# Seven block products for the last product of both layers of a decoder trunk, with the low halves of the weights made by adding DMAs

## The chip, the core and the metric

The kernel runs on one core of one Trainium2 chip. The metric is the device time of one execution in microseconds, the median of 3 runs. TensorE (PE) multiplies, VectorE (DVE), ScalarE (ACT) and GpSimd (POOL) do the elementwise work, and DMAs are started from SP's queue and from POOL's queue. All arithmetic is float32; a product of two float32 matrices is made of three products of "float32r" halves (below).

## The reference, cut to what matters

Two layers over x (1024 tokens by 1024 channels), each with a norm that is modulated by a vector c, a mixer, and a gated sum with x. Only the end of each mixer concerns the change:

```python
def even_mixer(h, ...):                       # layer 0
    ya = rg_lru(causal_depthwise_conv(xa, conv_w, conv_b), ...) * jax.nn.silu(ga)
    ...
    yb = stick_breaking_attention(q, k, v).reshape(bsz, slen, SB_WIDTH) * jax.nn.silu(gb)
    return jnp.concatenate([ya, yb], axis=-1) @ w_out          # 2048 x 1024

def odd_mixer(h, ...):                        # layer 1
    u, g = jnp.split(h @ w_in, 2, axis=-1)
    y = jax.nn.gelu(s5_ssm(u, ...))
    y = y * jax.nn.sigmoid(y @ glu_w + glu_b)
    return (y * jax.nn.silu(g)) @ w_out                        # 1024 x 1024
...
    x = x + gate * out                        # after each layer
```

In layer 0, `concatenate([ya, yb]) @ w_out` is the sum of a product with ya and one with yb, each 1024 x 1024 x 1024. The SSM of layer 1 needs rotation tables (powers of complex numbers on the unit circle, 32 of them by 128 steps on 128 partitions), which depend on parameters alone.

## The kernel before, in words

Activations lie feature by token: eight tiles of 128 features by 1024 tokens. A product with a 1024 x 1024 weight is made in eight output tiles m ("projections"). Each factor is split into a high half (a cast to float32r, line 72, on ACT) and a low half (the value less its high half, line 75, on DVE), and for each of eight k there are six matmuls of 512 tokens (lines 120 to 125): high weight by high and low activation, low weight by high activation, for two halves of the tokens. So a projection is 48 matmuls, and a whole product 384. A weight tile comes by SP into `w_raw` (two buffers), is split into `w_hi`, `w_lo` (two buffers each), and `w_next` asks for one tile ahead. The low half of the tile for projection m+2 can only be made once projection m has ended.

A second way of making a 1024 x 1024 product stands at the end of layer 1 (lines 1495 to 1559). Weights and activations are cut into 2 x 2 blocks (weights by even and odd output tile pairs, tokens in two halves), seven sums or differences of blocks are multiplied instead of eight blocks, and the results are put together (a Strassen-Winograd form). For each pair of output tiles u = 0..3 there are seven products of 4 x 3 matmuls (`st_mm`, lines 197 to 199): 84 matmuls, 336 in all. `st_x` (line 150) makes the seven right factors of a pair j of activation tiles: four differences on DVE, high halves on ACT, low halves on DVE. `st_w` (line 168) makes the seven left factors of u: sums and low halves on POOL (lines 181 to 189), high halves on ACT. For u = 0 the products run interleaved, j by j, in seven PSUM banks; for u > 0 one after the other.

Layer 0 ends in `out_even`: eight projections with ya, then eight with yb, each followed by `residual` (line 1159: x1 tile plus gate times the bank, two DVE instructions). yb comes back from DRAM in eight pieces through the `w_raw` buffers and is split. Beside the projections with yb, each finished x1 tile is scaled and split for layer 1 (lines 1181, 1182), stored by POOL's queue (1184) and squared for the next norm (1189, 1190). Eight `rotations` (line 1204 on) build the rotation tables on DVE, four instructions to a level, levels of 1, 2, 4, ... columns, in chunks of at most 32, and store them by POOL's queue.

PE's order is the order of the code. On the other engines a scheduler sets the order, except at the very start of the program, which is written out (a "manual schedule" names engines that take the order of the code). An engine waits at the head of its queue; what stands behind waits too.

Of the kernel before, what the change touches and what calls it, by code (L numbers as in the profile page):

```python
# [17 lines left out]
P = 128  # L18
# [32 lines left out]
GB = 2  # L51
LRU_ORDER = "gt0 ga1 cv1 cv2 ga2 gt1 dc0 cv3 gt2 ga3 xa4 cv4 gt3 dc0 xa5 cv5 gt4 xa6 cv6 ga4 gt5 dc0 xa7 cv7 gt6 ga5 gt7 dc0 ga6 ga7"


class Trunk:
# [33 lines left out]
    def shifted(self, raw):  # L89

        v = self.nc.vector
        out = self.h1p.tile([P, P], F32, name="wsh", tag="wsh", bufs=2)
        self.wsh.append(out)
        for k in range(KT):
            x, s = raw[:, k * P:(k + 1) * P], self.mod[:, 24 + k:25 + k]
            if k == 0:
                v.tensor_scalar(out, x, s, 0.0, op0=ALU.mult, op1=ALU.add)
            else:
                v.scalar_tensor_tensor(out, x, s, out, op0=ALU.mult, op1=ALU.add)

    def w_fetch(self, n):

        while self.w_loaded < min(len(self.w_order), n):
            hi = self.wp.tile([P, 1024], F32R, name="w_hi", tag="whi", bufs=2)
            lo = self.wp.tile([P, 1024], F32R, name="w_lo", tag="wlo", bufs=2)
            raw = self.load_split(self.w_order[self.w_loaded], hi, lo)
            if self.w_loaded in self.w_shifted:
                self.shifted(raw)
# [41 lines left out]
    def st_x(self, hi, lo, a, b, t):  # L150
# [3 lines left out]
        b2 = b.rearrange("p (c n) -> p c n", c=2)  # L154
        v.tensor_sub(t[:, 0], a[:, h1], a[:, h0])
        act.copy(hi[:, 0], a[:, h0])
        v.tensor_sub(t[:, 2], b[:, h1], a[:, h1])
        act.copy(hi[:, 1:3], b2)
        v.tensor_sub(t[:, 1], b[:, h1], t[:, 0])
        v.tensor_sub(t[:, 3], b[:, h0], t[:, 1])  # L160
        v.tensor_sub(lo[:, 0], a[:, h0], hi[:, 0].bitcast(F32))
        v.tensor_sub(lo[:, 1:3], b2, hi[:, 1:3].bitcast(F32))
        for i in (0, 2, 1, 3):
            act.copy(hi[:, 3 + i], t[:, i])
            v.tensor_sub(lo[:, 3 + i], t[:, i], hi[:, 3 + i].bitcast(F32))

    def st_w(self, src0, src1, place, t):

        nc = self.nc
        act, pool = nc.scalar, nc.gpsimd  # L170
        a = []
        for src in (src0, src1):
            raw = self.rp.tile([P, 1024], F32, name="w_raw", tag="raw")
            nc.sync.dma_start(raw, src)
            r = raw.rearrange("p (j e m) -> p e j m", e=2, m=P)
            a += [r[:, 0], r[:, 1]]
        s1, s2, s3, s4 = t[:, 0], t[:, 1], t[:, 2], t[:, 3]
        out = []
        for i, x in enumerate((a[0], s2, a[1], s3, s1, a[3], s4)):
            if i == 1:  # L180
                pool.tensor_tensor(s1, a[2], a[3], op=ALU.add)
                pool.tensor_tensor(s2, s1, a[0], op=ALU.subtract)
            elif i == 3:
                pool.tensor_tensor(s3, a[0], a[2], op=ALU.subtract)
            elif i == 6:
                pool.tensor_tensor(s4, a[1], s2, op=ALU.subtract)
            hi, lo = place(i)
            act.copy(hi, x)
            pool.tensor_tensor(lo, x, hi.bitcast(F32), op=ALU.subtract)
            out.append((hi, lo))  # L190
        return out
# [32 lines left out]
    def run(self):  # L224
# [12 lines left out]
        for half in range(2):  # L237
            self.w_order += [I["woe"][m][:, half * 1024:(half + 1) * 1024] for m in range(8)]
        self.s5_order = self.plan_s5()
        self.w_odd, self.w_shifted, self.wsh = len(self.w_order), set(), []  # L240
# [903 lines left out]
    def out_even(self):  # L1144
        nc, I = self.nc, self.I
        v = nc.vector
        x1p = self.pool("x1")
        x1 = self.x1 = x1p.tile([P, KT, T], F32, name="x1")
        ybp = self.pool("yb")
        ybh = ybp.tile([P, KT, T], F32R, name="yb_hi")  # L1150
        ybl = ybp.tile([P, KT, T], F32R, name="yb_lo")
        self.pair_i = 3
        ya = (self.yah, self.yal)

        def residual(m, ps):
            gate = self.mod[:, 16 + m:17 + m]
            for h in range(2):
                hs = slice(h * 512, (h + 1) * 512)
                v.scalar_tensor_tensor(x1[:, m, hs], ps[h], gate, x1[:, m, hs], op0=ALU.mult, op1=ALU.add)
# [3 lines left out]
        for m in range(8):  # L1163
            residual(m, self.proj(self.pair(), self.w_next(), ya))
            self.load_split(self.yb_s[m], ybh[:, m, :], ybl[:, m, :])
        self.yap2.release()
        self.yap.release()
        op = self.pool("oe")
        acc = op.tile([P, T], F32, name="acc")
        self.rot_s = [self.tc.dram_tile([P, 2, 4, P], F32, name=f"rot_s{m}") for m in range(8)]  # L1170
        self.h1p = self.pool("h1", side="right")
        self.h1h = self.h1p.tile([P, KT, T], F32R, name="h1_hi")
        self.h1l = self.h1p.tile([P, KT, T], F32R, name="h1_lo")
        self.rstd1 = self.h1p.tile([P, T], F32, name="rstd1")
        self.w_shifted.update(range(self.w_odd, self.w_odd + 3))
        self.x1_s = [self.tc.dram_tile([P, T], F32, name=f"x1_s{m}") for m in range(8)]
        for m in range(8):
            ps = self.proj(self.pair(), self.w_next(), (ybh, ybl))
            residual(m, ps)
            g = self.gain[:, 8 + m:9 + m]  # L1180
            nc.scalar.activation(self.h1h[:, m, :], x1[:, m, :], AF.Identity, scale=g)
            v.scalar_tensor_tensor(self.h1l[:, m, :], x1[:, m, :], g, self.h1h[:, m, :].bitcast(F32),
                                   op0=ALU.mult, op1=ALU.subtract)
            nc.gpsimd.dma_start(self.x1_s[m], x1[:, m, :])
            if m == 0:
                nc.scalar.activation(acc, x1[:, m, :], AF.Square)
            else:
                sq = op.tile([P, T], F32, name="sq1", tag="sq")
                nc.scalar.activation(sq, x1[:, m, :], AF.Square)
                v.tensor_add(acc, acc, sq)  # L1190
            self.rotations(m, op)
        self.acc = acc
        self.oe_pools = (op, ybp)
# [445 lines left out]
```

## Time and profile before

| | |
|---|---|
| three runs | 1343.68, 1343.10, 1342.44 us, median 1343.1 |
| the profiled execution | 1343.34 us, of which the span of the profile is 1341.3 us |
| PE busy | 1316.6 us (98%), 7020 matmuls, granted clock 0.999 |
| DVE, ACT, POOL busy | 1010.6, 651.8, 228.9 us |
| projections with ya, with yb | start at 767.5 and 856.2 us; the next product starts at 943.3 us |
| seven-product stage at the end | 1257.0 us to 1337.0 us |

The profiled execution lies 0.24 us above the median and 2.0 us above its own span. Busy shares are averages; a change in one stage is read from the rows of that stage. A matmul of 512 columns is listed with about 390 ns because its end is modelled; the distance from one start to the next is the pace.

### The profile page before, as it was taken

The numbers are of one execution on the slowest core, as the hardware profiler recorded it, in microseconds if no ns is written. First come the engines' busy times: TensorE is split into PE (matmuls) and PEld (weight loads), VectorE is DVE, ScalarE is ACT, GpSimd is POOL, SyncE is SP. The second block draws the span as 40 slices with busy tenths as digits, with TensorE's granted clock in tenths as the row PEclk, the third lists the DMA queues.
The fourth block names the chain that finished last, engine by engine and source line by source line (L and its number), as shares of the span: only waits on it lengthen the run. The fifth ranks groups of instructions, "written<-read, shape, count | busy, mean of one in ns | idle before, by whom it ended". The sixth has DMA issues, their size and how long they took to land.

```text
span 1341.3 us, 18939 instructions
## 1 busy us (share of the span) xinstructions
PE 1316.6 (98%) x7020; PEld 1137.7 (85%) x7020; DVE 1010.6 (75%) x1826; ACT 651.8 (49%) x1218; POOL 228.9 (17%) x411
## 2 busy tenths in 40 slices
PE   7998999999999999999999999999999999999998
PEld 3898989898999999988878878888888888888777
DVE  7949977777787868787999787866588669755653
ACT  6545454545454545455998621132463434632421
POOL 1012322222222222210000000000000000000784
PEclk9999999999999999999999999999999999999999
DMA  8443141414141414213112164342458778444331
GB/s 324 166 149 95 58 142 37 146 34 145 34 145 34 147 33 158 85 63 110 36 40 67 61 230 136 115 145 99 135 164 247 229 246 245 122 163 133 108 112 76
DMA packets 73356, 168.22 MB, mean 125 GB/s; under 512 B 9552, under 2 KB 35408, under 8 KB 73264
## 3 DMA queue, kind: packets, MB, share of 16 engines
q1 hardware_dynamic: 62256, 128.40, 31.3%
q0 software_dynamic: 11008, 38.62, 7.8%
q8 instruction: 55, 0.90, 0.3%
q14 instruction: 37, 0.30, 0.1%
HBM read 126.16 MB, written 40.83 MB: 125 GB/s over the span
## 4 chain that ended last, share of the span: by engine, by line
PE 78%; DVE 13%; ACT 3%; issue 3%; DMA 2%; POOL 1%; DVEq 0%; ACTq 0%; POOLq 0%
PE bank L120 6%; PE bank L121 6%; PE bank L123 6%; PE bank L122 6%; PE bank L124 6%; PE bank L125 6%; PE bank L771 6%; PE bank L773 6%; PE bank L772 6%; PE bank L837 2%; PE bank L199 2%; PE bank L197 2%; PE bank L198 2%; DMA ada_raw<-ada 2%; PE bank L849 1%
## 5 line engine op out<-in xcount | busy, mean ns | idle before, releaser
L771 PE MATMUL bank<-wqkv_hi,h_hi 128*128 128x384 f32 x512 | 173.6, 339 | 0.0
L773 PE MATMUL bank<-wqkv_hi,h_lo 128*128 128x384 f32 x512 | 172.3, 337 | 0.0
L772 PE MATMUL bank<-wqkv_lo,h_hi 128*128 128x384 f32 x512 | 172.3, 337 | 0.0
L72 ACT CAST w_hi<-w_raw 128x1024 fp32r<-128x1024 f32 x60 | 63.0, 1050 | 193.5 <-PE bank L123 148.5
L75 DVE TENSOR_TENSOR w_lo<-w_raw,w_hi 128x1024 fp32r<-128x1024 f32 x60 | 73.0, 1218 | 41.2 <-ACT w_hi L72 41.1
L771 PEld LDWEIGHTS bank<-wqkv_hi,h_hi 128*128 128x128 f32 x512 | 96.6, 189 | 0.3
L772 PEld LDWEIGHTS bank<-wqkv_lo,h_hi 128*128 128x128 f32 x512 | 96.6, 189 | 0.4
L773 PEld LDWEIGHTS bank<-wqkv_hi,h_lo 128*128 128x128 f32 x512 | 96.5, 189 | 0.0
L120 PE MATMUL bank<-h_hi,w_hi 128*128 128x512 f32 x224 | 89.1, 398 | 0.0
L122 PE MATMUL bank<-h_hi,w_hi 128*128 128x512 f32 x224 | 87.6, 391 | 0.8 <-DVE xc L1014 0.8
L124 PE MATMUL bank<-h_hi,w_lo 128*128 128x512 f32 x224 | 87.7, 392 | 0.4 <-DVE w_lo L75 0.4
L121 PE MATMUL bank<-h_lo,w_hi 128*128 128x512 f32 x224 | 87.7, 391 | 0.0
L123 PE MATMUL bank<-h_lo,w_hi 128*128 128x512 f32 x224 | 87.5, 390 | 0.0
L125 PE MATMUL bank<-h_hi,w_lo 128*128 128x512 f32 x224 | 87.4, 390 | 0.0
L778 ACT ACTIVATE nat<-bank 128x128 f32<-128x128 f32 x64 | 17.7, 277 | 141.3 <-PE bank L773 137.9
L826 DVE TENSOR_TENSOR_SCAN keep<-keep,diag 128x1024 f32<-128x1024 f32 (+3 forms) x64 | 86.2, 1347 | 0.1
L314 POOL TENSOR_SCALAR ss<-ss 128x2 f32<-128x2 f32 x64 | 28.6, 446 | 296.6 <-ACT nat L779 296.1
L820 ACT ACTIVATE keep<-bank,ss 128x512 f32<-128x512 f32 (+2 forms) x96 | 54.5, 597 | 21.7 <-PE bank L819 20.1
L783 DVE SCALAR_TENSOR_TENSOR nat<-bank,ss,gqk 128x128 f32<-128x128 f32 x64 | 22.1, 345 | 47.9 <-PE bank L837 25.9
L823 ACT ACTIVATE beta<-bank,ss 128x512 f32<-128x512 f32 (+3 forms) x96 | 54.4, 600 | 0.0
L290 DVE SCALAR_TENSOR_TENSOR ada_raw<-ada_raw,cs 128x1024 f32<-128x1024 f32 x39 | 47.6, 1220 | 7.8 <-DMA ada_raw<-ada 7.5
L315 POOL TENSOR_TENSOR ss<-ss,mh 128x2 f32<-128x2 f32 x64 | 51.9, 810 | 5.3
(436 smaller groups left out, 3739.2 us busy)
## 6 DMA issues: line engine op xcount, KB each, us to landing
ada_raw<-ada SPq DMA_DIRECT2D x39, 512.0 KB, 3.9
w_raw<-wqkv SPq DMA_DIRECT2D x21, 512.0 KB, 3.6
w_raw<-wfm SPq DMA_DIRECT2D x20, 512.0 KB, 3.6
w_raw<-woe SPq DMA_DIRECT2D x16, 512.0 KB, 3.8
w_raw<-wod SPq DMA_DIRECT2D x16, 512.0 KB, 4.4
x<-xT SPq DMA_DIRECT2D x8, 512.0 KB, 7.1
cx_s<-ce POOLq DMA_DIRECT2D x16, 256.0 KB, 2.7
win_s<-wsb POOLq DMA_DIRECT2D x16, 256.0 KB, 3.5
```

Of the source, the lines that this page charges most:

```text
L72: nc.scalar.copy(hi, raw)
L75: nc.vector.tensor_sub(lo, raw, hi.bitcast(F32))
L120: nc.tensor.matmul(ps[0], wh[:, k, :], rh[k][:, h0], start=first, stop=False)
L121: nc.tensor.matmul(ps[0], wh[:, k, :], rl[k][:, h0], start=False, stop=False)
L122: nc.tensor.matmul(ps[1], wh[:, k, :], rh[k][:, h1], start=first, stop=False)
L123: nc.tensor.matmul(ps[1], wh[:, k, :], rl[k][:, h1], start=False, stop=False)
L124: nc.tensor.matmul(ps[0], wl[:, k, :], rh[k][:, h0], start=False, stop=last)
L125: nc.tensor.matmul(ps[1], wl[:, k, :], rh[k][:, h1], start=False, stop=last)
L771: nc.tensor.matmul(ps[:, 0:384], hh[:, k, ts], wqh[:, ks], start=(k == 0), stop=False)
L772: nc.tensor.matmul(ps[:, 0:384], hh[:, k, ts], wql[:, ks], start=False, stop=False)
L773: nc.tensor.matmul(ps[:, 0:384], hl[:, k, ts], wqh[:, ks], start=False, stop=(k == KT - 1))
L826: v.tensor_tensor_scan(rev, rev, self.diag[:, T - n:T][:, ::-1], 0.0, op0=ALU.mult, op1=ALU.max)
```

## The change

Layer 0's product with yb is now made of seven block products too, and both layers share one function, `strassen`. In it, and from one projection ahead of it, the order of DVE, ACT, POOL and SP is that of the code. For u = 0 five products (4, 5, 0, 1, 2) run interleaved over the first three j, then the rest; for u > 0 the order is 4, 5, 0, 1, 3, 2, 6. The sums of weight blocks are made on DVE. For the low half of a left factor ACT writes the high half, then the source once more with scale -1 into the low half's place (which is cast, so it holds the negative of the high half), and POOL's queue starts a DMA that adds the unsplit block onto it: from DRAM for plain blocks, from SBUF for sums. No compute instruction of POOL is left at the end of the program.

The activations' factors of layer 0 are made from yb directly: pairs 0 and 1 beside the projections with ya, pairs 2 and 3 around the last of them. The stores of x1 and of the output are started by SP instead of POOL (but for the last pair's). Layer 1's input product takes its halves from tiles that the factors leave free; three small products with the shift vector (`shifted`) get loads of their own. The rotation tables are built in batches: the first five levels for 16 at once (`rotations_small`), the last two for four at once without chunks, beside the projections with ya.

```diff
-    def st_x(self, hi, lo, a, b, t):
+    def st_x(self, z, a, b, t):
...
+        for i in range(7):
+            act.copy(z[i][:, 0], x[i])
+        for i in range(7):
+            v.tensor_sub(z[i][:, 1], x[i], z[i][:, 0].bitcast(F32))
     def st_w(self, src0, src1, place, t):
...
-            hi, lo = place(i)
-            act.copy(hi, x)
-            pool.tensor_tensor(lo, x, hi.bitcast(F32), op=ALU.subtract)
+        v.tensor_add(s1, a[2], a[3])
+        v.tensor_sub(s2, s1, a[0])
+        v.tensor_sub(s4, a[1], s2)
+        v.tensor_sub(s3, a[0], a[2])
+        x = ((a[0], d[0]), (s2, s2), (a[1], d[1]), (s3, s3), (s1, s1), (a[3], d[3]), (s4, s4))
...
+        def make(*factors):
+            for i in factors:
+                ws[i] = hi, lo = place(i)
+                hf, lf = [y.rearrange("p j m -> p (j m)") for y in (hi, lo)]
+                act.copy(hf, x[i][0])
+                act.activation(lf, x[i][0], AF.Copy, scale=-1.0)
+                nc.gpsimd.dma_start(lf, x[i][1], accum_op=ALU.add)
+    def strassen(self, base, first, w_load, x, tile, gate, scratch, during, after):
...
+        ws, make = first
+        for u in range(4):
...
+            if u == 0:
+                order = [(i, j) for j in range(3) for i in (4, 5, 0, 1, 2)] + [(i, 3) for i in (4, 5, 0, 1)]
+                order += [(3, j) for j in range(4)] + [(2, 3)] + [(6, j) for j in range(4)]
+                for i, j in order:
+                    self.st_mm(b[i], ws[i], x(i, j), j, j == 0, j == 3)
+                p1, p6, p2, p7, p5, p4, p3 = b
+            else:
+                make(3, 6)
+                after(u - 1)
...
+            product(4, p5)
+            product(5, p4)
+            product(0, p1)
+            add(xb[:, h1], p5, gb)
+            if u == 0:
+                add(xa[:, h1], p5, ga)
...
+            add(xb[:, h0], p4, gb)
+            if u < 3:
+                ws, make = w_load(u + 1)
+                during(u)
+                if u == 0:
+                    make(4, 5)
+                    nc.scalar.copy(s1, p1)
+                    make(0, 1, 2)
+                else:
+                    nc.scalar.copy(s1, p1)
+                    make(4, 5, 0, 1, 2)
...
+            product(1, p6)
+            v.tensor_add(u2, p6, s1)
...
+            product(3, p7)
...
+            product(2, p2)
+            add(xa[:, h0], p2, ga)
+            product(6, p3)
+            add(xa[:, h1], p3, ga)
+        after(3)
     def out_even(self):
...
+        for m in range(6):
             residual(m, self.proj(self.pair(), self.w_next(), ya))
...
+            if m in (0, 1):
+                yb_factors(m)
+            if m in (1, 3):
+                small[m // 2] = self.rotations_small(m // 2, rotp)
+            for r in ((), (0, 1), (2, 3), (4, 5), (6,), (7,))[m]:
+                self.rotations(r, rotp, small[r // 4])
...
+        with self.tc.manual_schedule(engines={eng.DVE, eng.Activation, eng.Pool, eng.SP}):
+            first = w_load(0)
+            first[1](4, 5, 0, 1, 2)
+            self.proj(p7, w7, ya)
...
+            yb_factors(2)
+            residual(7, p7)
+            first[1](3, 6)
+            yb_factors(3)
+            self.strassen(0, first, w_load, x, lambda m: x1[:, m, :], gate,
...
     def layer1(self):
...
+            first = w_load(0)
+            first[1](4, 5, 0, 1, 2)
+            self.proj(p7, w7, (yh, yl))
+            sg = gate_tile(7)
+            z_factors(2)
+            v.tensor_mul(y[:, 7, :], gated(7, p7), sg)
+            first[1](3, 6)
+            z_factors(3)
+            self.strassen(4, first, w_load, x, tile, lambda m: self.mod[:, 40 + m:41 + m], lambda: scratch("x"),
```

What the scheduler makes of DVE beside the second and third projection with ya: before, the sums of projection 1 (banks 71 and 72), then the weight's low half for projection 3, then pieces of a rotation (`rot`).

```order
L1159 SCALAR_TENSOR_TENSOR x_7271<-bank_71,mod,x_7271 128x512
L1159 SCALAR_TENSOR_TENSOR x_7271<-bank_72,mod,x_7271 128x512
L75 TENSOR_TENSOR w_lo<-w_raw,w_hi 128x1024
L1216 TENSOR_TENSOR rot_7954<-rot,uw 128x8x8
L1217 TENSOR_TENSOR rot_7955<-rot,uw 128x8x8
L75 TENSOR_TENSOR yb_lo<-w_raw,yb_hi 128x1024
```

And now, at the same place of DVE's queue; `yb_raw` are the two yb tiles of pair 1, `st_x` their differences, `z` the right factors.

```order
L1260 SCALAR_TENSOR_TENSOR x_7271<-bank_71,mod,x_7271 128x512
L1260 SCALAR_TENSOR_TENSOR x_7271<-bank_72,mod,x_7271 128x512
L155 TENSOR_TENSOR st_x<-yb_raw_7439 128x512
L156 TENSOR_TENSOR st_x<-yb_raw_7441,yb_raw_7439 128x512
L157 TENSOR_TENSOR st_x<-yb_raw_7441,st_x 128x512
L162 TENSOR_TENSOR z<-yb_raw_7439,z 128x512
L158 TENSOR_TENSOR st_x<-yb_raw_7441,st_x 128x512
L162 TENSOR_TENSOR z<-yb_raw_7441,z 128x512 x2
L162 TENSOR_TENSOR z<-st_x,z 128x512 x4
L1398 TENSOR_TENSOR rot<-rot_7495,rot_7496 128x4x32
L76 TENSOR_TENSOR w_lo<-w_raw,w_hi 128x1024
```

The same low half `w_lo` now stands behind the eleven instructions for the factors of pair 1 and a piece of a rotation.

POOL at the beginning of layer 1's seven products, before: sums (`st_w`) and low halves computed.

```order
L181 TENSOR_TENSOR st_w<-w_raw 128x512
L184 TENSOR_TENSOR st_w<-w_raw 128x512
L182 TENSOR_TENSOR st_w<-st_w,w_raw 128x512
L189 TENSOR_TENSOR w_lo<-st_w,w_hi 128x512
L189 TENSOR_TENSOR w_lo<-w_raw,w_hi 128x512
L186 TENSOR_TENSOR st_w<-w_raw,st_w 128x512
```

And now: DMAs that add a sum (`st_w`) or a block of the weight in DRAM (`woo`).

```order
L191 DMA w_lo<-st_w 128x512
L191 DMA w_lo<-woo 128x512 x2
L191 DMA w_lo<-st_w 128x512
L191 DMA w_lo<-woo 128x512
L191 DMA w_lo<-st_w 128x512 x3
```

The subtractions have left POOL; in their place are transfers, of which the first five belong to u = 0's products 4, 5, 0, 1, 2.

DVE ahead of layer 1's first products, now: the gating of activation tile 6, the product of gate 7 with its activation (`gsr`), the factors of pair 2, and only then the gating of tile 7.

```order
L1680 TENSOR_TENSOR x_7271<-sgl,gsr 128x1024
L1674 TENSOR_TENSOR gsr<-gsr,x_7271 128x1024
L155 TENSOR_TENSOR st_x<-x_7271 128x512
L156 TENSOR_TENSOR st_x<-x_7271 128x512
L157 TENSOR_TENSOR st_x<-x_7271,st_x 128x512
L158 TENSOR_TENSOR st_x<-x_7271,st_x 128x512
L162 TENSOR_TENSOR z<-x_7271,z 128x512 x3
L162 TENSOR_TENSOR z<-st_x,z 128x512 x4
L1714 TENSOR_TENSOR x_7271<-sgl,gsr 128x1024
```

`gsr` has one buffer instead of two, so its load for tile 7 waits until tile 6 is gated, and everything below it in this list waits for that load.

## Rows read from the trace of the kernel before

**Rows 1.** The page, part 1: busy time, share of the span, instructions.
```profile
span 1341.3 us, 18939 instructions
...
PE 1316.6 (98%) x7020; PEld 1137.7 (85%) x7020; DVE 1010.6 (75%) x1826; ACT 651.8 (49%) x1218; POOL 228.9 (17%) x411
```
**Rows 2.** Busy time by stretch, matmuls alone: projections with yb, seven-product stage.
```profile
core 0: us, PE busy (x) PEld busy (x) DVE busy (x) ACT busy (x), PEclk, DMA share, GB/s
856.23:943.32 87.09, 87.09 (x386) 72.07 (x384) 11.29 (x17) 0.00 (x0) 1.00 0.32 109
1257.01:1337.04 80.03, 77.98 (x337) 62.76 (x335) 18.00 (x25) 3.60 (x6) 1.00 0.33 104
```
**Rows 3.** Timeline of PE: start, length, instruction. First u = 0, then u = 3.
```profile
1262.05 0.39 PE L199 MATMUL bank<-z_hi,w_lo 128*128 128x512 f32 x1
...
1266.85 0.39 PE L199 MATMUL bank<-z_hi,w_lo 128*128 128x512 f32 x1
...
1332.65 0.39 PE L199 MATMUL bank<-z_hi,w_lo 128*128 128x512 f32 x1
...
1336.81 0.40 PE L199 MATMUL bank<-z_hi,w_lo 128*128 128x512 f32 x1
```
**Rows 4.** Timeline of PE: where it waits in the seven-product stage.
```profile
1259.18 0.50 PE L199 MATMUL bank<-z_hi,w_lo 128*128 128x512 f32 x1 [0.85 <-POOL w_lo L189]
...
1279.15 0.50 PE L199 MATMUL bank<-z_hi,w_lo 128*128 128x512 f32 x1 [1.21 <-POOL w_lo L189]
```
**Rows 5.** Timeline of PE: the projections with ya begin, and their one wait.
```profile
767.47 0.40 PE L120 MATMUL bank<-ya,w_hi 128*128 128x512 f32 x1
...
778.07 0.50 PE L121 MATMUL bank<-ya_slot,w_hi 128*128 128x512 f32 x1 [0.57 <-DVE rot L1205]
```
**Rows 6.** Timeline of DVE beside projections 1 and 2 with ya.
```profile
777.97 0.06 DVE L1204 MEMSET rot<- 128x4 f32 x1
...
780.23 0.18 DVE L1216 TENSOR_TENSOR rot<-rot,uw 128x32 f32<-128x32 f32 x1
...
780.85 0.23 DVE L1216 TENSOR_TENSOR rot<-rot,uw 128x64 f32<-128x64 f32 x1
...
781.57 0.29 DVE L1216 TENSOR_TENSOR rot<-rot,uw 128x128 f32<-128x128 f32 x1
...
783.81 0.43 DVE L1216 TENSOR_TENSOR rot<-rot,uw 128x256 f32<-128x256 f32 x1
...
785.13 0.43 DVE L1216 TENSOR_TENSOR rot<-rot,uw 128x256 f32<-128x256 f32 x1
...
793.28 1.40 DVE L1159 SCALAR_TENSOR_TENSOR x<-bank,mod,x 128x512 f32<-128x512 f32 x2
794.92 1.23 DVE L75 TENSOR_TENSOR w_lo<-w_raw,w_hi 128x1024 fp32r<-128x1024 f32 x1 [0.24 <-ACT w_hi L72]
```
**Rows 7.** Timeline of DVE while right factors are made, POOL idle, then POOL at work.
```profile
1197.97 1.89 DVE L165 TENSOR_TENSOR z_lo<-st_x,z_hi 128x512 fp32r<-128x512 f32 x3
...
1256.71 4.66 DVE L165 TENSOR_TENSOR z_lo<-st_x,z_hi 128x512 fp32r<-128x512 f32 x4
```
**Rows 8.** Groups of ACT and DVE by shape: busy us, mean ns, idle before.
```profile
L188 ACT CAST w_hi<-st_w 128x512 fp32r<-128x512 f32 x16 | 9.7, 619 | 24.8 <-POOL st_w L182 14.1 <-POOL st_w L186 6.6 <-PE bank L198 3.2
...
L1504 DVE SCALAR_TENSOR_TENSOR x<-bank,mod,x 128x512 f32<-128x512 f32 x18 | 13.2, 747 | 18.2 <-PE bank L199 17.4 <-ACT st_x L1517 0.7
```
**Rows 9.** DMA issues: queue, count, KB each, median us from issue to landing.
```profile
w_raw<-yb_s SPq DMA_DIRECT2D x8, 512.0 KB, 3.8
...
win_s<-wsb POOLq DMA_DIRECT2D x16, 256.0 KB, 3.5
...
gsr<-gs_s SPq DMA_DIRECT2D x8, 512.0 KB, 4.4
...
out<-x POOLq DMA_DIRECT2D x7, 512.0 KB, 5.2
...
out<-x POOLq DMA_DIRECT2D x1, 256.0 KB, 2.3
```

More of the change, by code (lines that the diff above doesn't have):

```diff
@@ new lines, in st_w, with st_places, place @@
+        return ws, make
+    def st_places(self, pool):
+        two = {}
+        def place(i):
+            if i in (2, 4, 5):
+                return [pool.tile([P, 4, P], F32R, name=f"w{i}_{x}", tag=f"w{i}_{x}", bufs=1 + (i == 2)) for x in ("hi", "lo")]
+            k = i // 3
+            if k > 0:
+                k, i = 1, i // 6
+            if k not in two:
+                two[k] = [self.wp.tile([P, 2, 4, P], F32R, name=f"w_{x}", tag=f"w{x}", bufs=2) for x in ("hi", "lo")]
+            return [x[:, i] for x in two[k]]
+        return place
@@ L1164, in out_even @@
+        small = {}
+        for m in range(6):
             residual(m, self.proj(self.pair(), self.w_next(), ya))
[L1165 to L1172, printed above, removed]
@@ L1322, in s5_in @@
             v.memset(rho[:, :, 0:1], 0.0)
-            L = sp.tile([P, 2, 4, P], F32, name="L", tag="L")
+            L = place("L", [P, 2, 4, P])
             for ri in range(2):
@@ L1360, in s5_load @@
         def s5_load(m):
-            cx = sp.tile([P, 4, 2, P], F32, name="cx", tag="cx")
+            cx = place("cx", [P, 4, 2, P])
             for ri in range(2):
@@ L1374, in s5_out @@
             u = us.pop(m)
-            yn = late.tile([P, 8, P], F32, name="yn", tag="yn")
+            yn = place("yn", [P, 8, P])
             for hf in range(2):
@@ L1387, in s5_out @@
                 s5_load(m + 1)
-            yts[m] = yt = late.tile([P, T], F32, name="yt", tag="yt")
+            yts[m] = yt = place("yt", [P, T])
             nc.sync.dma_start(yt.rearrange("p (j k) -> p j k", j=8), ys.rearrange("j c g k -> (c g) j k"))
@@ L1392, in s5_gelu @@
             yt = yts.pop(m)
-            t = late.tile([P, T], F32, name="gt", tag="gt")
+            t = place("gt", [P, T])
             nc.scalar.activation(t, yt, AF.Square)
@@ L1559, in layer1 @@
                 nc.sync.dma_start(self.out[6][:, h1], xa[:, h1])
-        for p in (zp, fp, yhp, self.x1p, self.wp, self.rp, self.cp):
+        w7 = self.w_next(ahead=0)
+        p7 = self.pair()
+        eng = mybir.EngineType
+        with self.tc.manual_schedule(engines={eng.DVE, eng.Activation, eng.Pool, eng.SP}):
+            first = w_load(0)
[7 more added lines that the diff above has]
+            self.strassen(4, first, w_load, x, tile, lambda m: self.mod[:, 40 + m:41 + m], lambda: scratch("x"),
+                          lambda u: None, after)
+        for p in (self.zpool[1], fp, yhp, self.zpool[0], self.x1p, self.wp, self.rp, self.cp):
             p.release()
```

383 lines of the change are left out of this document (211 added, 172 removed).

## The prediction, made before the result was known

> **What bounds the kernel now.** I read the page's busy shares first, then the stretches of the two products that the change is about, then PE's timeline for its waits, then DVE, ACT and the DMA list for what could take their place. PE is busy 98% of the span, DVE 75%, ACT 49%, POOL 17% [rows 1]: the time is the sum of PE's matmuls, and another engine matters only where PE has to wait for it. In the projections with yb nothing waits at all: 384 matmuls in 87.09 us, 0.227 us each [rows 2]. The seven-product stage takes 80.03 us for 336 matmuls [rows 2]. Its pace is not quite that of the projections: in u = 0, 21 matmuls in 4.80 us, 0.229 each; in u = 3, 18 in 4.16 us, 0.231 each [rows 3]. The rest of that stage is two visible waits for a low half made on POOL, 0.85 and 1.21 us, with the restart behind each [rows 4]. The clock is granted in full in both stretches, so paces can be carried from one to the other.
>
> **Layer 0: 48 matmuls less.** Seven products of 12 matmuls, four times, are 336 in place of 384. At the pace of the stage that already works so, 84 x 0.229 + 252 x 0.231 = 19.2 + 58.2 = 77.5 us. Against 87.1 us that is -9.6 us, not the 48 x 0.227 = 10.9 us of a bare count. It is PE time with no wait in it, so it comes off the end in full, if the new stage isn't held up.
>
> **Layer 1: the waits for POOL go.** The stage has the same 336 matmuls. Without waits it is 77.5 us too, against 80.0: 2.5 us can be won. The sums move to DVE, and the right factors, which DVE makes there, no longer run beside POOL: three low halves of 128x512 take 1.89 us with POOL idle, four take 4.66 us with POOL at work [rows 7], 0.63 against 1.17 us each.
>
> What is late next there? Call T the end of the last gated projection. Tile 6 is gated after projection 6 ends at T-10.9: a cast of 0.6 that waits for the weight buffer of projection 6, two sigmoids of 0.6, a DVE product of 1.2, so T-7.9. Only then may the gate of tile 7 be loaded, into its one buffer: 4.4 us [rows 9], T-3.5. DVE has this product behind it (1.2), then eleven instructions for pair 2 at 0.6 each (6.6, T+4.3), the gating of tile 7 (1.2), four differences (2.4, T+7.9) and seven low halves (4.2, T+12.1). PE reaches the fourth j of product 5, which needs the last of these, after 49 matmuls: T+11.2. So a wait of 0.9 us stays, between 0 (the load in 3.5 us) and 3 us (each handover from ACT to DVE 0.1 us more, the load 5). Layer 1 by this: 80.0 to 78.4, -1.6 us.
>
> The same chain in layer 0 has its inputs from DRAM earlier. DVE there: residual of tile 6 until T-9.5, four weight sums (2.4), four differences and seven low halves for pair 2, bounded by ACT's ten weight casts and seven activation casts at 0.62 [rows 8], until about T+1.5; residual 7 (1.4); pair 3's second yb tile, loaded after the third low half of pair 2 (3.8 us [rows 9]), about T+2.6; then eleven instructions of 0.6 until T+9.5. Needed at T+11.2: room of 1.7 us, cost 0.
>
> **The rotations and pair 1: a new wait.** The scheduler has put the low half for projection 3 behind the factors of pair 1 on DVE; before, it came right behind the residual and was started at 794.92 [rows 6]. Now from the same beginning, 777.97 [rows 6], DVE does: the first five levels for 16 tables, of which the starts in [rows 6] give 0.6, 0.7, 1.3 for 32, 64 and 256 columns, about 0.9 for 128, and for 512 I add two instructions of 0.6 and two of 0.43: 2.1, together 5.6 us; inside them residual 0 (1.4) and a low half (1.2): 786.2. Then the first two products of a rotation, which wait for a copy by ACT: 1.6, to 787.8. Pair 0: eleven of 0.6 and a piece of a rotation: 6.9, to 794.7. Residual 1: 1.4. Pair 1: 6.9, 803.0. Then the low half: 804.2. PE starts projection 3 after 767.47, its old wait of 0.74, and three projections of 11.0 us (eight take 88.76 - 0.74 [rows 2, 5]), 801.2, and uses a low weight at its fifth matmul, 802.1. So a wait of 2.0 us: 0 at best (if the rotation batches run as fast as the 0.06 to 0.2 us instructions around them), 4 at worst, if each of the 22 factor instructions waits 0.1 us for ACT. I take 2.0. From there on DVE has 11 us for each projection and less to do (two batched rotations are some 7 us), so later low halves are in time.
>
> **The adding DMAs.** No row shows one. What the trace has is plain transfers of POOL's queue: 256 KB in 2.3 and 3.5 us, 512 KB beside other traffic in 5.2 us [rows 9]. What hides them: a factor is needed at a block's start plus its place in the order. In u = 0 of layer 0 ACT is through with factors 4 to 2 between T-7.5 and T-3.5, and PE needs their low halves between T+0.5 and T+3.2: room of 8.0 down to 6.7 us. Between blocks 0 and 1 it is tight: DVE can first read the bank of product 4 at T+11, three additions of 0.75 [rows 8], one sum (0.6), two ACT instructions (1.2): T+15.1, and PE needs the low half of factor 4 at T+19.7. Room 4.6 us; in layer 1, with DVE at T+12.1, 4.5 us. Between later blocks it is 8 us and more. A transfer that reads as much again should stand between 3.5 and 5.2; I take 4.8, which costs 0.2 us at each of the two tight places, 0.4 together. Ends: 0 at 2.3 us, 1.3 at 5.2.
> The Trainium skill, Collectives: The Full Stack, section "The bandwidth ceiling: the fold count and why AG ≠ RS ≠ AR", says that an add in the DMA path costs no cycles of its own but needs two source reads, which halves its rate. With DMA: Bandwidth & Descriptors, section on the anatomy of a DMA (2.0 us and bytes at 436 GB/s), an estimate is 2.0 + 2 x 0.6 = 3.2 us, and the cost would be 0 instead of 0.4. The trace's 3.5 us for a plain 256 KB is already above it, so I stay with the rows.
>
> **What else moves.** SP now holds the stores of finished tiles at the head of its queue until their last sum; behind them stand the weight loads of the next block, which DVE needs some 6 us into the block, while the store goes about 5 us after the block's start at latest: 0, at worst 2 us. The squares and the norm's sums sit on ACT and DVE ahead of the next block's first additions; product 3 of block 1 overwrites the bank that these read, 11 us into the block, and they end about 10 us into it: 0, at worst 1.5. At the end of layer 0 the last two x1 tiles are split about 4 us after PE's last matmul there and needed 8 us after it: 0. The tail (last matmul, one addition, one store) is as before.
>
> **The sum.** -9.6 + 2.0 - 1.6 + 0.4 = -8.8 us. The profiled execution (1343.34 us, span 1341.3) would become 1334.5; it lies 0.24 above the median of the runs, so the median becomes 1343.1 - 8.8 = 1334.3 us.
>
> **Rivals.**
> A. All new waits are covered: DVE keeps up beside the projections, the gate's load is quick, the transfers are short. -9.6 - 2.5 = -12.1, 1331.0 us. For it: DVE's idle share of 25%. Against: both chains above have no slack in their own sum. 15%.
> B. The adding transfers are slow. The places are the starts of block 1 in both layers (room 4.6, 4.5 us) and of block 0 in layer 0 (6.7 us); in all other blocks from about 8 us on. With a landing time L the cost is (L-4.6) + (L-4.5) + (L-6.7), which eats the 9.2 us of gain without it at L = 8.3. At 10 us these three cost 12.1 and the other blocks some 1.5 us each, six of them: 1343.1 - 9.2 + 21 = 1355 us. For it: each transfer both reads and writes its place, there are seven in 19 us, and POOL's queue runs them in turn. Against: no 256 KB row above 3.5 us. 13%.
> C. The written order costs more than the sums show: each engine now stands still for its own queue's head, where a scheduler had packed it. If the waits on DVE's chains double and the moved queues cost their worst, 2.0 + 0.9 + 2 + 1.5 on top: 1334.3 + 6.4 = 1340.7 us. For it: three places with under 2 us of room. Against: after the first block of a layer DVE has under 15 us of work in 19. 14%.
> That the change doesn't do what it says can be left out: the order of PE's instructions shows 48 matmuls less.
>
> **The numbers.** The forecast holds 58%. 0.2% is about what a measurement of this kernel can tell from no change, 2.7 us: faster means below 1340.4. Forecast and A are faster, and half of C and a fifth of B: 0.82. No change: the other half of C and a little of B: 0.07. Slower, the rest of B and mishaps of C: 0.11. The range goes from 1329 (A with layer 1 unchanged and its pace a little better) to 1342, which leaves B's slow part out; the likeliest case alone is 1331 to 1338.
>
> **What would show it.** PE's stretch from the first to the last product of layer 0 near 77.5 us, at 0.229 and then 0.231 us per matmul; one wait of about 2 us of PE for `w_lo` about 34 us after the projections with ya begin; no row of PE waiting for POOL's arithmetic; a wait under 2 us for a right factor at the fourth j of layer 1's block 0; the adding transfers with 3 to 5.5 us to landing. Wrong would be: transfers above 7 us with PE waiting for low halves at the starts of blocks; PE waiting for banks (`x<-bank`) inside the blocks; more than 5 us of waits before T in layer 0.

## The result and the profile after

The changed kernel takes 1352.4 us (median of 7 runs, 1347.8 to 1355.5) against 1343.7 us for the kernel before, measured beside it (7 runs): a ratio of 1.0059, with a 95% interval of 1.0039 to 1.0080. Some 9 us were to be won, 9 were lost. The profiled execution of the changed kernel was the slowest of its seven (1355.5 us, 3.1 above the median), and that of the plain copies below is the fastest of its twelve (1338.9 us, 2.4 under the median), so their lengths in the table differ by 5.5 us more than their medians do.

The page of the changed kernel: PE is busy longer than before [rows 1], with 48 matmuls less.

```profile
span 1353.5 us, 18993 instructions
...
PE 1318.2 (97%) x6972; PEld 1131.7 (84%) x6972; DVE 1025.0 (76%) x1744; ACT 699.2 (52%) x1330; POOL 203.7 (15%) x409
```

The stretches from its first to its last seven-product stage (columns as in [rows 2] and POOL, but here every instruction is counted, where [rows 2] has only those that touch a bank; POOL's in the products are the issues of its DMAs): layer 0's product, what lies between, layer 1's product.

```profile
858.58:948.56 89.98, 82.39 (x338) 64.88 (x337) 66.55 (x103) 46.28 (x76) 19.84 (x23) 0.96 0.76 193
948.56:1264.83 316.27, 315.83 (x1692) 261.20 (x1690) 219.14 (x253) 144.30 (x199) 20.29 (x29) 1.00 0.61 180
1264.83:1348.20 83.37, 79.98 (x337) 63.87 (x335) 44.68 (x64) 32.16 (x61) 21.08 (x25) 0.98 0.77 201
```

Each length, from first matmul to first matmul (the last product's to its end), against the forecast and two of the experiments below, the plain copies and the last version of all:

| us | before | forecast | changed | plain copies | last version |
|---|---|---|---|---|---|
| projections with ya | 88.8 | 90.8 | 90.4 | 90.4 | 88.8 |
| layer 0's product | 87.1 | 77.5 | 90.0 | 80.0 | 79.3 |
| between | 313.7 | 313.7 | 316.3 | 317.4 | 316.4 |
| layer 1's product | 80.0 | 78.4 | 83.3 | 78.4 | 78.3 |

The granted clock is no longer full in the two products, and the DMA engines, a third busy there before [rows 2], are busy three quarters of the time. PE's timeline has the new waits (start, length, instruction; in brackets the wait and what ended it), the first in the projections with ya, five in layer 0, three in layer 1:

```profile
804.45 0.50 PE L123 MATMUL bank<-ya,w_lo 128*128 128x512 f32 x1 [1.30 <-DVE w_lo L76]
...
861.51 0.50 PE L301 MATMUL bank<-z,w_lo 128*128 128x512 f32 x1 [0.23 <-DMA w_lo<-st_w]
...
865.23 0.50 PE L301 MATMUL bank<-z,w_lo 128*128 128x512 f32 x1 [2.77 <-DMA w_lo<-woeb]
...
903.53 0.50 PE L301 MATMUL bank<-z,w_lo 128*128 128x512 f32 x1 [0.36 <-DMA w_lo<-st_w]
...
925.24 0.50 PE L301 MATMUL bank<-z,w_lo 128*128 128x512 f32 x1 [1.60 <-DMA w_lo<-st_w]
...
938.69 0.76 PE L299 MATMUL bank<-z,w_hi 128*128 128x512 f32 x1 [2.52 <-DVE x L219]
...
1269.04 0.50 PE L301 MATMUL bank<-z,w_lo 128*128 128x512 f32 x1 [0.83 <-DMA w_lo<-woo]
...
1305.93 0.50 PE L301 MATMUL bank<-z,w_lo 128*128 128x512 f32 x1 [0.57 <-DMA w_lo<-st_w]
...
1327.59 0.80 PE L301 MATMUL bank<-z,w_lo 128*128 128x512 f32 x1 [1.99 <-DMA w_lo<-st_w]
```

The wait of 2.52 us ends with DVE's addition out of a bank. Seven of the eight in the two products end with the landing of an adding DMA; together the eight are 10.9 us. They cost more than they show. Behind the wait of 2.77 us the clock is granted at half (1.2 instead of 2.4 GHz) for eight matmuls. Windows of that place: the third column from the end is the granted clock.

```profile
865.50:867.10 1.60, 1.60 (x7) 1.26 (x7) 0.95 (x2) 0.80 (x2) 0.00 (x0) 0.90 0.95 339
867.10:870.30 3.20, 3.20 (x9) 2.50 (x8) 3.17 (x6) 2.93 (x6) 0.00 (x0) 0.52 1.08 307
870.30:873.00 2.70, 2.70 (x14) 2.19 (x13) 2.70 (x5) 0.00 (x0) 0.00 (x0) 1.00 0.62 148
```

A matmul takes 0.427 us there instead of 0.23, so this adds 1.6 us; behind the waits of 2.52 and 1.99 us the same happens for some seven matmuls each, about 1.5 us. Behind the shorter waits of this trace it does not. The granted clock of this whole execution is 0.994, that of the other six 0.996 to 1.000, so most of them have less of it.

Why is a low half late at the start of block 3 of layer 0 (923.00)? The chain of waits (start, length, what; pieces under 0.1 us are left out) leads back into block 2, which began at 902.54:

```profile
909.54 1.24 DVE acc L1320
...
910.80 0.78 ACT sq L1319
911.58 8.08 DMA w_raw<-woeb
...
919.78 0.70 DVE st_w L178
...
920.63 0.40 issue
921.03 0.63 ACT w_lo L190
```

The first two pieces stand ahead of the load in time, but SP did not wait for them: its queue waited 14.8 us for DVE's last sum of a finished tile, until 908.38, and then started two stores and two loads in turn. The second weight tile of block 3 is asked for 9 us into block 2 and lands 8.1 us later; DVE's sum, ACT's two instructions and the first adding DMA, issued at 922.01 and landed at 925.19, follow. PE wants it at 923.5. In the DMA list (KB each, median us to landing) the same loads, 3.6 us in layer 1 before, are:

```profile
w_lo<-st_w POOLq DMA_DIRECT2D x32, 256.0 KB, 6.2
...
w_raw<-woeb SPq DMA_DIRECT2D x8, 512.0 KB, 7.5
...
w_raw<-woo SPq DMA_DIRECT2D x8, 512.0 KB, 10.1
```

So a single adding transfer is not slow (3.2 us when it is the first of its group); a group of them is, and so is everything issued behind it.

### The profile page after: what moved, and what is told of

Read it like the earlier page. It is cut to its first block, busy times and chain, and to the rows that moved or that the text cites. A ratio compares the mean times of both kernels' runs of the same rounds, so it can differ in the third digit from the quotient of the medians.

```text
span 1353.5 us, 18993 instructions
## 1 busy us (share of the span) xinstructions
PE 1318.2 (97%) x6972; PEld 1131.7 (84%) x6972; DVE 1025.0 (76%) x1744; ACT 699.2 (52%) x1330; POOL 203.7 (15%) x409
## 4 chain that ended last, share of the span: by engine, by line
PE 61%; DVE 20%; DMA 7%; ACT 5%; issue 4%; POOL 1%; SPq 0%; DVEq 0%; ACTq 0%; POOLq 0%
PE bank L872 5%; PE bank L874 5%; PE bank L873 5%; PE bank L119 3%; PE bank L121 3%; PE bank L120 3%; PE bank L122 3%; PE bank L124 3%; PE bank L123 3%; PE bank L938 2%; PE bank L301 2%; DMA ada_raw<-ada 2%; PE bank L299 2%; PE bank L300 2%; DMA w_raw<-woo 1%
## 5 line engine op out<-in xcount | busy, mean ns | idle before, releaser
L73 ACT CAST w_hi<-w_raw 128x1024 fp32r<-128x1024 f32 x52 | 54.5, 1047 | 133.2 <-PE bank L122 87.8
L76 DVE TENSOR_TENSOR w_lo<-w_raw,w_hi 128x1024 fp32r<-128x1024 f32 x52 | 63.4, 1219 | 48.0 <-ACT w_hi L73 47.7
L301 PE MATMUL bank<-z,w_lo 128*128 128x512 f32 x224 | 90.8, 405 | 8.3 <-DMA w_lo<-st_w 4.7
L299 PE MATMUL bank<-z,w_hi 128*128 128x512 f32 x224 | 90.6, 405 | 2.6 <-DVE x L219 2.5
L300 PE MATMUL bank<-z,w_hi 128*128 128x512 f32 x224 | 89.4, 399 | 0.0
L123 PE MATMUL bank<-h_hi,w_lo 128*128 128x512 f32 x224 | 87.1, 389 | 0.4 <-DVE w_lo L76 0.4
L301 PEld LDWEIGHTS bank<-z,w_lo 128*128 128x128 f32 x224 | 43.1, 192 | 21.5 <-DMA w_lo<-st_w 6.9
```

The costliest lines, as they stand in the source:

```text
L123: nc.tensor.matmul(ps[0], wl[:, k, :], rh[k][:, h0], start=False, stop=last)
L299: mm(ps, wh[:, j], xh, start=start, stop=False, skip_group_check=True)
L300: mm(ps, wh[:, j], xl, start=False, stop=False, skip_group_check=True)
L301: mm(ps, wl[:, j], xh, start=False, stop=stop, skip_group_check=True)
```

## The experiments

Theories: **T1**, adding transfers keep the DMA engines busy about twice as long as plain ones, and loads and later low halves queue behind them; **T2**, the loads are asked for too late, behind stores that wait for DVE; **T3**, the latency of a transfer from POOL's queue; and rival C of the prediction, DVE's written order.

**Plain copies in place of the adds.**

```
- nc.gpsimd.dma_start(lf, x[i][1], accum_op=ALU.add)
+ nc.gpsimd.dma_start(lf, x[i][1].bitcast(F32R))
```

> The adding DMAs become plain DMAs of the same 256 KB from the same sources to the same places (the low half then holds the whole value, so that part of the computation is left out). Theory T1, the adding transfers take up the DMA engines (in the changed kernel a landing every 1.3 us for 256 KB that adds, and the same 1.3 us for 512 KB that does not), and the weight loads behind them land 7 to 10 us after issue: weight loads back at 4 to 5 us, PE's waits for low halves at the starts of blocks gone with the half-clock stretches behind them, about 1340 us. Theory T2, the loads are issued too late (SP holds the stores of finished tiles ahead of them until DVE's last sums, 5 to 6 us into a block) and the adding costs little: only the wait of 2.8 us in block 0 of layer 0 goes, about 1347. Theory T3, the fixed latency of a transfer on POOL's queue (3.2 us and 1.04 us between issues) is what PE waits for: no change, about 1352.

Measured: 1341.3 us (12 runs), 11.1 below the changed kernel, ratio to the kernel before 0.9979 (0.9967 to 0.9990). Nothing but the addition inside the DMA was taken away: number, size, ends and queue of the transfers are the same. PE waits for a low half from a DMA once, 0.27 us in block 0. That is T1's time, but the weight loads did not fall to 4 or 5 us: in the two layers they land in 6.0 and 7.1 us (7.5 and 10.1 with the adds); each block's stores and loads still go out together. Its DMA list:

```profile
w_lo<-st_w POOLq DMA_DIRECT2D x32, 256.0 KB, 2.7
w_lo<-woeb POOLq DMA_DIRECT2D x12, 256.0 KB, 3.0
w_lo<-woo POOLq DMA_DIRECT2D x12, 256.0 KB, 3.1
```

A stretch of 7 us of the changed kernel (883 to 890) in which the engines move adding transfers alone, in 40 slices: share of the engines in tenths, then GB/s, then the mean.

```profile
DMA  7799967979987999999999999899999999999999
GB/s 129 140 176 222 199 105 129 152 129 187 176 129 129 176 176 223 222 187 211 187 199 211 176 199 187 164 176 176 222 187 187 199 211 222 199 211 199 211 199 222
DMA packets 695, 1.28 MB, mean 183 GB/s; under 512 B 73, under 2 KB 73, under 8 KB 694
```

The engines are full at 183 GB/s. With plain copies, the same stretch holds only SP's plain transfers, and they get 343:

```profile
DMA  0599999999999999497955989999998899999999
GB/s 0 234 398 398 421 374 398 398 468 422 374 374 421 374 257 281 94 304 70 305 211 211 374 328 421 468 375 351 328 375 304 328 374 445 445 398 375 492 374 374
DMA packets 650, 2.40 MB, mean 343 GB/s; under 512 B 64, under 2 KB 64, under 8 KB 650
```

The page's DMA queues (packets, MB, share of 16 engines) say the same of POOL's queue: the changed kernel, plain copies, and, from the experiment with DVE below, the queue without the 56 transfers.

```profile
q0 software_dynamic: 17056, 45.96, 12.7%
```

```profile
q0 software_dynamic: 17056, 45.96, 10.1%
```

```profile
q0 software_dynamic: 8992, 31.28, 6.3%
```

Times the spans (1353.5, 1336.9, 1347.3 us) that is 171.9, 135.0 and 84.9 us: 1.55 us of all engines for each adding transfer, 0.90 for each plain one. Seven adds are 10.9 us in a block of 19.5. T1 holds, with 1.7 times the time for an add; T3 falls, since the plain transfers had the same queue and start.

The Trainium skill, Collectives: The Full Stack, section "The bandwidth ceiling: the fold count and why AG ≠ RS ≠ AR", says of a collective, ReduceScatter, that its add needs two source reads and so gets half the rate of AllGather, which copies. The trace agrees in direction: 183 against 343 GB/s, but these 343 are SP's loads and stores; for the same transfers with and without the add it is 1.55 against 0.90 us, a factor of 1.7.

**POOL subtracts.**

```
- act.activation(lf, x[i][0], AF.Copy, scale=-1.0)
- nc.gpsimd.dma_start(lf, x[i][1], accum_op=ALU.add)
+ nc.gpsimd.tensor_tensor(lf, x[i][0], hf.bitcast(F32), op=ALU.subtract)
```

> Low halves of the left factors by POOL's subtraction (value less high half), no second ACT instruction, no adding DMA; all else as in the changed kernel. T1: DMA traffic of a block falls by more than half, weight loads land in 4 us, the waits for low halves at blocks 2 and 3 go; DVE is somewhat slower beside POOL: about 1341 us. T2: loads still issued 5 to 6 us into a block, so blocks 2 and 3 start late as now; 1347. T3: a subtraction of about 1.2 us replaces 3.2 us to landing, 1340 to 1343.

Measured: 1365.3 us, ratio 1.0156 (1.0139 to 1.0173). All three expectations were wrong: the DMA traffic fell, layer 1's product took 81.8 us, but layer 0's 103.9. PE now waits for DVE to free banks, up to 6.57 us in block 3, and some 29 matmuls of layer 0's product run at half clock, about 6 us:

```profile
951.52 0.77 PE L298 MATMUL bank<-z,w_hi 128*128 128x512 f32 x1 [6.57 <-DVE x L218]
```

Beside POOL the sums for the shift vector (seven instructions on DVE, 128x128) take 7.25 us; in the changed kernel, where POOL computes nothing, 2.68. First the kernel with POOL's subtraction, then the changed one:

```profile
879.89 7.25 DVE L100 SCALAR_TENSOR_TENSOR wsh<-wsh_raw,mod,wsh 128x128 f32<-128x128 f32 x7
```

```profile
879.94 2.68 DVE L100 SCALAR_TENSOR_TENSOR wsh<-wsh_raw,mod,wsh 128x128 f32<-128x128 f32 x7
```

It is the effect of [rows 7], on an engine that has no room for it. The Trainium skill, SBUF — State Buffer, section "Who interferes with whom", says that a DVE instruction with two SBUF inputs contends with a GpSimd instruction that reads SBUF. The trace agrees: 1.04 against 0.38 us from one to the next.

**Loads ahead of the stores.**

```
  make(3, 6)
+ raws = w_raws(u + 1) if u < 3 else None
  after(u - 1)
```

> Adding DMAs kept; in SP's queue the two weight loads of the next block stand ahead of the stores of the finished tiles (blocks 1 and 2 of both layers), so they are issued 3 to 5 us earlier. T2: the waits for low halves at blocks 2 and 3 go, 1343 us. T1: the loads are issued into the middle of the seven adding transfers and land some 3 us earlier only; part of the gain, 1346 to 1349. T3: no change, 1352.

Measured: 1349.7 us, 2.8 below the changed kernel, ratio 1.0044 (1.0028 to 1.0059): nearest to T1, though the interval overlaps with the changed kernel's. Layer 0's product 84.3, layer 1's 81.8 us. The loads of block 2 are asked for 0.7 us after the first adding DMA and land in 4.6 and 7.3 us, in the midst of the group; the adds land later in turn (median of those from sums 7.5 instead of 6.2 us). Asking earlier gave back a quarter of the 11.1 us.

**DVE subtracts.**

```
- act.activation(lf, x[i][0], AF.Copy, scale=-1.0)
- nc.gpsimd.dma_start(lf, x[i][1], accum_op=ALU.add)
+ v.tensor_sub(lf, x[i][0], hf.bitcast(F32))
```

> Low halves of the left factors by DVE's subtraction, at 0.6 us each, in the place of the adding DMAs; no POOL and no DMA in it. T1 and T2 as for the subtraction on POOL, but DVE carries 4.4 us more in every block and stands behind ACT's casts: 1341 to 1346 us under T1, 1348 under T2. If the written order of DVE is the limit (rival C of the prediction), it becomes slower than the changed kernel's 1352.

Measured: 1349.1 us, ratio 1.0039 (1.0023 to 1.0054): not slower than the changed kernel, and by the time alone nearest to T2's 1348. The trace says otherwise: PE waits for a low half once, 0.33 us. In layer 1 this is all that is wanted: 78.8 us. In layer 0 (88.1 us) DVE is too full: PE waits 0.97, 2.29 and 2.02 us in blocks 1 to 3 for DVE to free a bank, the first of them here:

```profile
891.74 0.47 PE L298 MATMUL bank<-z,w_hi 128*128 128x512 f32 x1 [0.97 <-DVE x L218]
```

So rival C has its place here, in layer 0 alone, where DVE also makes layer 1's input halves and the sums of the norm.

**The order of the input tiles.** The stretch between the products is 2.6 us longer than before, with the same matmuls and less waiting (one wait of 0.44 us, before one of 1.02). In 75 us of the projections for the gate PE is at 333 matmuls before and at 327 after the change, those under way at both ends counted (us, PE busy and count, granted clock, DMA share, GB/s):

```profile
1175.00:1250.00 75.00, 75.00 (x333) 1.00 0.41 135
```

```profile
1175.00:1250.00 75.00, 75.00 (x327) 1.00 0.35 114
```

The program places the halves of an activation elsewhere now: tiles alternate between the lower and the upper part of a partition.

```
+ K_H1 = (0, 2, 4, 6, 1, 3, 5, 7)    # input projections: tiles below 128 KiB first
+ K_Y = (0, 2, 6, 4, 5, 1, 3, 7)     # projections for the gate
- for k in range(k0, k1):
+ for k in ks:
```

> The changed kernel with one edit: in layer 1's input projections and in the projections for the gate the eight input tiles are taken in another order, first those that the program has placed in the lower 128 KiB of each partition, then those above (the sums are the same, in another order). Theory P: PE's pace depends on where the moving tiles lie. In the traces so far, stages whose tiles all lie below that address have 0.2267 us per matmul, those all above it 0.2289, and those that alternate between the two 0.231; the change made these two stages alternate. Then the pace there falls to about 0.228, and the stretch between the two seven-product stages from 316.3 us to 313 or 314. Rival: the pace of 0.231 is left behind by PE's waits or by DMA traffic in the stage before; then it stays 0.231 and the stretch 316. In the whole time 2 to 3 us at most, 1350.

Measured: 1351.1 us. The pace went the way that theory P wanted, to 0.229 us per matmul from the first projection in the new order on (half of the tiles lie low, so 0.228 was expected), 0.231 as ever in the two products, whose tiles still alternate. The stretch did not get shorter (318.6 us): in its first projection the order asks for tiles that are made last, and PE waits 1.57, 0.61 and 0.62 us for them.

**A mixture.** Adds only where they hide, the rest by DVE; loads first; in layer 0's last block `during(0)` behind the addition that frees product 5's bank; pair 1's factors one projection later.

```
+ if i in dma:  # layer 0: 4, 5, 0, 1, 3, 6 for u = 0, then 1, 2, 3, 6; layer 1: 4, 5 for u = 0
      act.activation(lf, x[i][0], AF.Copy, scale=-1.0)
      nc.gpsimd.dma_start(lf, x[i][1], accum_op=ALU.add)
+ else:
+     v.tensor_sub(lf, x[i][0], hf.bitcast(F32))
- if m in (0, 1):
-     yb_factors(m)
+ if m in (0, 2):
+     yb_factors(m // 2)
```

> Adding DMAs kept only where they hide: in layer 0 six of seven factors of block 0 and factors 1, 2, 3, 6 of later blocks, in layer 1 factors 4 and 5 of block 0; the other low halves by DVE. The next block's weight loads ahead of the stores in SP's queue; in layer 0's last block the halves for layer 1 behind the addition that frees a bank; pair 1's factors one projection later, so that the low half for projection 3 is ahead of them. T1 (the adding transfers fill the DMA engines): layer 0's stage 80 to 82 us, layer 1's 78.5, no wait in the third projection: 1339 to 1341 us. Rival (the written order of DVE is the limit): waits of 1 to 2 us for banks in each block of layer 0 as with DVE's subtraction, 1346.

Measured: 1343.4 us (12 runs), ratio 1.0008 (0.9995 to 1.0020), above T1's 1339 to 1341. The wait in projection 3 is gone (88.8 us), blocks 1 to 3 of layer 0 take 19.48 us each, without a wait, layer 1's product 78.7, so the rival's waits for banks did not come. But block 0 of layer 0 takes 24.2 us. DVE's one low half there is of the factor that ACT makes last, and DVE stands still for it:

```profile
856.58 0.69 DVE L200 TENSOR_TENSOR w_lo<-w_raw,w_hi 128x512 fp32r<-128x512 f32 x1 [5.00 <-ACT w_hi L195]
```

**The same, without adds.**

> As the mixture, but every low half by DVE and no adding DMA at all. If DVE has room with the new order: 1340 us, as the mixture. If DVE is the limit in layer 0 (4.2 us more in each block than with adding DMAs): layer 0's stage 84 to 86 us, 1345.

Measured: 1346.1 us, ratio 1.0026 (1.0017 to 1.0034). Layer 0's product took 82.0 us, better than expected, but DVE then is late for the next projection: PE waits 3.79 us for a bank at its start.

**The mixture in the new order of tiles.**

> The mixture and the order of the input tiles by address together. By theory P 2 to 3 us below the mixture, 1337 to 1338 us; by its rival the same as the mixture.

Measured: 1347.9 us, ratio 1.0028 (1.0016 to 1.0040): 4.5 above the mixture, which neither side expected. The pace was 0.229 again, and the waits of the first try came with it (1.57, 0.62, 0.60); in this execution PE also waited 3.04 us for a bank at the end of layer 0, against 0.84 in the mixture, and some 15 matmuls ran at half clock, about 3 us.

**The mixture mended.** Factors 4, 5, 0 by DVE and 1, 2, 3, 6 by adding DMAs, in all of layer 0 and block 0 of layer 1; later blocks of layer 1 by DVE.

> As the mixture, with the choice of who makes which low half set by its trace: in all blocks of layer 0 and in block 0 of layer 1 factors 4, 5 and 0 by DVE (their high halves are ACT's first, so DVE no longer stands 5 us behind ACT's ninth instruction in block 0 of layer 0), factors 1, 2, 3, 6 by adding DMAs; later blocks of layer 1 all by DVE. If that standing still made block 0's waits: block 0 of layer 0 from 24.2 to 21.5 us, the other blocks 19.5, the whole 1340 to 1341 us. If DVE's amount of work made them: block 0 stays at 24, 1343.

Measured: 1338.8 us, ratio 0.9967 (0.9954 to 0.9980). Block 0 of layer 0 fell to 22.3 us, so the standing still made 1.9 of the 4.7 us that it had above the other blocks. Its waits for low halves (0.98 and 0.28 us) are gone; those for right factors (1.52 and 0.84) stayed, for which DVE waits 1.67 us for a tile of yb to land. Of the 4.5 us between the two traces, 1.6 lie ahead of the projections with ya, where nothing was edited.

**And in the new order, from the fifth input projection on.**

```
+ u_out(m, self.proj(mm_pair(), self.w_next(), h1, K_H1 if m > 3 else None))
```

> The same and the order of the input tiles by address, but only from the fifth input projection on (in the earlier try the order asked for late tiles in the fourth, which cost PE 2.8 us of waits) and in the gate's projections. Theory P: the stretch between the two seven-product stages 2 to 2.5 us shorter than in the kernel beside it, 1338 us. Rival (pace without effect on the end): the same time.

Measured: 1336.6 us (1335.4 to 1337.9, 5 runs) against 1343.0, ratio 0.9948 (0.9935 to 0.9960): the fastest of all, though its interval overlaps with that of the version before it. PE is at 329 matmuls in the 75 us of above. In the traces 0.9 us lie in the stretch between the products (316.4 against 317.3 us, with 0.6 us more of waits), not the 2 to 2.5 expected, and 1.5 in block 0 of layer 0, which the edit doesn't touch. That the order of tiles changes the pace is shown three times; what it is worth in the time lies between 0.9 us and the 2.2 of the medians, and most of the 2.2 isn't shown to be its work. Its products, columns as above:

```profile
856.69:935.96 79.27, 78.38 (x338) 62.88 (x336) 70.11 (x111) 41.97 (x67) 12.01 (x14) 1.00 0.69 187
935.96:1252.40 316.44, 314.63 (x1692) 261.04 (x1690) 222.34 (x258) 142.57 (x196) 17.68 (x26) 1.00 0.60 178
1252.40:1330.67 78.27, 77.85 (x337) 62.83 (x335) 57.55 (x85) 21.59 (x40) 2.82 (x4) 1.00 0.42 138
```

## Why the prediction was wrong

Forecast 1334.3 us, measured 1352.4: 18.1 us. In the trace layer 0's product is 12.5 us over its forecast, layer 1's 4.9, the stretch between 2.6, all else 1.4, less the 0.4 that the sum held for the adds: 21.0, and the trace lies 3.1 above the median. By the steps of the prediction:

- **The adding DMAs, +0.4: the step that failed.** They cost 11.1 us (changed kernel less plain copies). The landing of one transfer, taken as 4.8 us, was too long if anything: the first of each group lands in 3.2 to 3.5. What failed is the sentence "Between later blocks it is 8 us and more". It has no working; a room of 8 us fits weight loads at the speed of [rows 9], while in the runs the adding transfers of the block before still held the DMA engines. Loads landed 7.5 and 10.1 us after issue, and the first low half of layer 0's block 2 was issued 2.2 us before that block, not 8. With plain copies it was 5.2 us, enough for a transfer that lands in 2.2. The prediction's own sign of being wrong came true: transfers of over 7 us, up to 10.8, with PE waiting for low halves at the starts of blocks. At the place that was called tight, between blocks 0 and 1, nothing waited: issued at 879.27, landed at 882.45, needed at 883.5, as worked out. I had priced a latency where the traffic of a whole block had to be summed: seven adds at 1.55 us and five plain transfers of 512 KB at 1.3 (the distance of their landings) are 17.4 of 19.5 us, and the loads of one block stand behind the adds of the block before. (At 4.8 us the two places would also have cost 0.2 and 0.3, not 0.2 each.)
- **Rival B** had nearly the time (1355 against 1352.4), the cause in its first half ("reads and writes its place", "seven in 19 us"), and in the main the wrong places: it lost most at the starts of block 1 in both layers, where the kernel lost nothing; the kernel lost at blocks 0, 2 and 3. Its sum has two slips that nearly cancel: at 10 us its three places cost 14.2, not 12.1, and the other blocks are five, not six; so 1355.6. That its time came so near is luck. A chance of 13% was too little: [rows 9] bounded one transfer's landing, not a group's.
- **What else moves, 0, at worst 2.** The loads behind the stores: 2.8 us, by the experiment that put them first. The halves for layer 1 ahead of an addition in the last block: a wait of 2.52 us and some seven half-speed matmuls behind it, about 3.9 us, gone in the mixture, which moves them, but also with plain copies, which don't: the adds were needed for it. Both overlap the 11.1. The tail, held to be as before, is 1.1 us longer in this trace and 0.1 shorter in the last version's.
- **Layer 0, -9.6.** Undisturbed blocks behind the first take 19.48 us, where the sum had 19.4; the last version's stage is 79.3 us, so the term is -7.8. Most of what is missing lies in block 0, 20.8 us against 19.2, with a wait of 0.85 us for a right factor at the fourth j, where the prediction saw room of 1.7 us.
- **Layer 1, 78.4 us.** Right where the adds don't disturb it (in the changed kernel it takes 83.3): 78.4 with plain copies, 78.3 in the last version, with the wait at the fourth j of product 5 where it was put (0.49 us against 0.9, in the trace of the plain copies):

```profile
1265.95 0.50 PE L300 MATMUL bank<-z,w_hi 128*128 128x512 f32 x1 [0.49 <-DVE z L162]
```

- **The wait in projection 3, +2.0.** Right in place and cause, 1.30 us in size (its own sum gives 2.1); it went when pair 1 was moved behind the low half.
- **Not in the prediction at all:** the pace of the matmuls between the products, +2.6 us, and the half clock behind long waits, about 4.6 us in the profiled execution, less in most others.

With the adds made plain the forecast would still have been 7 us too low (1341.3 against 1333.9 without its 0.4): 2.5 in layer 0 and 3.7 between the products; ahead of them its trace is 1.7 us under the forecast, but that trace lies 2.4 below the median.

## What to carry to other kernels

Where work is given to DMAs, sum the traffic of a period against the engines' time in it, with an adding transfer at the time that was measured for it (here 1.7 times a plain one), and then ask when the loads that share those engines land; the latency of one transfer tells nothing of this. When a matmul stage is paced by nothing but itself, a change that only moves its operands can still change its pace, so compare matmuls per microsecond in stages that the diff doesn't mention. And an engine that follows a written order loses time where its next instruction needs what another engine makes last: give it what is made first.

## What the runs showed that I had not expected

- DMA engines that do nothing but add move 183 GB/s, plain ones 343 in the same place.
- PE's pace with 512 columns has three levels, and they go with the place of the moving tiles in a partition, which the built program tells: all below 128 KiB 0.2267 us (projections with yb before), all above 0.2289 (projections with ya), alternating 0.231 (u = 3 in [rows 3]). Taking the same tiles sorted by place moved two stages from 0.231 to 0.229 at full granted clock. Why the place matters is open, and where in a partition the border lies: 128 KiB fits the tiles here, and no run tried others.
- A wait of PE of about 2 us or more was followed by half clock for seven or eight matmuls in three of three cases in the changed kernel, but not after 2.51 us in the first try with another order of tiles, nor after 2.02 us where DVE subtracts: a stall can cost 1.5 us beyond its length, and doesn't always.
- Seven small sums on DVE took 2.7 times as long while POOL subtracted (five of them 1.27 us each, against 0.35).
